# Down projections by seven products over 12 of 22 inner chunks, with squares at each eviction

## The chip, the cores and the metric

The kernel runs on one core of one Trainium2 chip. Its time is the device time of one execution in microseconds; less is better. The engines are TensorE (PE, with its weight loads as PEld), VectorE (DVE), ScalarE (ACT), GpSimd (POOL) and SyncE (SP), each of which takes its instructions in a fixed order from its own queue. DMAs are issued from the queues of SP and of POOL.

## The reference

A trunk of two layers over 512 tokens of width 1024, in float32:

```python
for i in range(DEPTH):                       # DEPTH = 2
    h = h + 0.5 * swiglu(rmsnorm(h, norm_ffn1[i]), ffn1_w_gate[i], ffn1_w_up[i], ffn1_w_down[i])
    hn = rmsnorm(h, norm_mix[i])
    h = h + (ab_mixer(hn, ...) if i % 2 == 0 else c_mixer(hn, ...))
    h = h + 0.5 * swiglu(rmsnorm(h, norm_ffn2[i]), ffn2_w_gate[i], ffn2_w_up[i], ffn2_w_down[i])
    gate = jax.nn.sigmoid(rmsnorm(h, norm_ple[i]) @ w_ple_gate[i])
    h = h + gate * (p[i] @ w_ple_proj[i])
return rmsnorm(h, norm_final)

def swiglu(x, w_gate, w_up, w_down):         # w_gate, w_up: 1024 x 2816, w_down: 2816 x 1024
    return (jax.nn.silu(x @ w_gate) * (x @ w_up)) @ w_down
```

The change is in the product with `w_down`, of which there are four (two in each layer), and in the RMS norm behind it.

## The kernel before

Activations lie transposed: a chunk is 128 features by 512 tokens, so `h` has 8 chunks (KC) and the inner activation of a feed-forward block 22 (NF). To keep float32 accuracy with the faster fp32r matmul, each operand is split into a high part (a copy rounded to fp32r, made by ACT) and a low part (the rest, made by DVE); `split` does this (L149, L150 for weights). A product is then three matmuls: high by high, high by low, low by high. Raw weights come by DMA into `wr` tiles; the split ones stand in the pools `whi` and `wlo`, of four buffers each, which set how far ahead weights can be prepared.

A feed-forward block computes its 22 inner chunks one after the other, with the gate and up products; the chunks' parts are kept in SBUF (the list `a`), and the raw chunks that the down projection needs again are written to DRAM (`raw`). Then `down` makes the 8 output chunks in four pairs m = 0, 2, 4, 6, every one over 22 inner chunks. The pair m = 0 is plain: 22 × 3 matmuls of 128x512 for each output chunk (L438 to L440). Beside it, `inner_sums` makes differences of inner chunks k and k + 4 for the later pairs (L515). The pairs 2, 4 and 6 treat the inner chunks 0 to 7 as 2 × 2 blocks (an output pair by two halves of 256 tokens) by a scheme of seven products in place of eight (Strassen's in Winograd's form). Its matmuls are 128x256 (L476 to L478); `inner_weights` makes the sums of weights on DVE (L529 to L533) and splits them. The products go to the banks p1, p2 (`mm`), y (`sc`) and z (`ob`); L490 to L494 combine y and z on DVE into two half results. The 14 other inner chunks are plain, behind the seven products, in each of these pairs.

At the end of an output chunk `evict` (L443) adds the PSUM bank to the residual on DVE and stores the new `h` to DRAM from POOL's queue (L444). For the next norm each chunk of `h` needs two things: its parts scaled by the gain (`norm_split`, L199 and L200), and its square (ACT, L207), which is added to the running sum `ssq` on POOL, or on DVE in the first norm and for the last chunk (L214). Chunks 3, 4 and 5 (LATER) were held back: SP fetches them again during the last pair, and both steps are done then.

At the very start `pair_front` does the first inner pairs of the first block, while the first norm is still being computed; PE sums `ssq` over partitions with one-column matmuls (L221), L223 and L224 make the inverse root of it, and L240 spreads it.

The order on each engine comes from a scheduler, which places the instructions by their dependences and its own estimates, in an order near that of the code; `issue_after` and `keep_in_program_order` tie single instructions.

Of the kernel before, what the change touches and what calls it, by code (L numbers as in the profile page):

```python
# [9 lines left out]
F32 = mybir.dt.float32  # L10
F32R = mybir.dt.float32r
# [4 lines left out]
P = 128  # L16
T = 512
# [19 lines left out]
SEVEN = 4  # L37
LATER = 3, 4, 5
UP_AT = 3
LEAD = 6  # L40
ACTS = 62
# [6 lines left out]
class Trunk:  # L48
# [155 lines left out]
    def norm_square(self, c):  # L204
# [5 lines left out]
        if c == 0:  # L210
            self.acc = sq
        else:
            eng = nc.vector if c == KC - 1 or self.k == 0 else nc.gpsimd
            eng.tensor_tensor(self.acc, self.acc, sq, op=ALU.add)  # L214
# [37 lines left out]
    def pair_front(self, w, m, first, ahead):  # L252
# [3 lines left out]
        for j in range(2):  # L256
            u = self.ahead.pop(0) if self.ahead else self.unit(w[:, (1 - j) * UNIT:(2 - j) * UNIT])
# [132 lines left out]
    def ffn(self, i, which, k_next):  # L390
# [8 lines left out]
        raw = self.dp.tile([2 * SEVEN, P, T], F32, name=self.nm("inner"))  # L399
        for m in range(NF):  # L400
# [6 lines left out]
            if m < 2 * SEVEN:  # L407
                nc.gpsimd.dma_start(raw[m], r)
# [9 lines left out]
    def down(self, w, a, raw, kept):  # L418

# [6 lines left out]
        later = []  # L426
# [6 lines left out]
        def plain(p, m, s, e, start):  # L433
            u = self.unit(w[m, :, s * P:e * P], (e - s) * P)
            for j, (xh, xl) in enumerate(a[s:e]):
# [4 lines left out]
                mm(p, u[1][:, c], xh, start=False, stop=s + j == NF - 1, skip_group_check=True)  # L440

        def evict(m, p, h):
# [10 lines left out]
        for s in range(0, NF, 8):  # L453
            for m in range(2):
                plain(ps[m], m, s, min(NF, s + 8), s == 0)
            if s == 0:
                sums = [self.inner_sums(k, a, raw) for k in range(SEVEN)]
# [3 lines left out]
        for m in range(2, KC, 2):  # L461
            hs = [fetched(m + j, kept) for j in range(2)]
            wa, wb, ws, wr = self.inner_weights(w[m, :, :UNIT], w[m + 1, :, :UNIT])
            M = UNIT // 2
            p1, p2, y, z = self.bank(), self.bank(), self.sbank(), self.obank()
            x11 = [(h[:, l], lo[:, l]) for h, lo in a[:SEVEN]]
            x21, x22 = [[(h[:, c], lo[:, c]) for h, lo in a[SEVEN:2 * SEVEN]] for c in (l, r)]
            t4 = [(h[:, r], lo[:, r]) for h, lo in a[:SEVEN]]
            t1, t2 = [[(h[:, c], lo[:, c]) for h, lo, _ in sums] for c in (l, r)]
            t3 = [(t[:, l], t[:, r]) for _, _, t in sums]  # L470

            def product(out, u, off, xs, start=False, stop=False):
                mm = nc.tensor.matmul
                for k, (xh, xl) in enumerate(xs):
                    c = slice(off + k * P, off + (k + 1) * P)
                    mm(out, u[0][:, c], xh, start=start and k == 0, stop=False, skip_group_check=True)  # L476
                    mm(out, u[0][:, c], xl, start=False, stop=False, skip_group_check=True)
                    mm(out, u[1][:, c], xh, start=False, stop=stop and k == SEVEN - 1, skip_group_check=True)  # L478

            e, f, u2 = self.tmp(), self.tmp(), self.tmp()  # L480
            product(y[:, l], wa, 0, x11, True)
            act(e[:, l], y[:, l], AF.Copy)
            product(p1[:, l], wa, M, x21, True)
            product(p2[:, l], wb, 0, t4, True)
            product(z[:, l], ws, M, t1, True, True)
            product(y[:, r], ws, 0, t3)
            product(p1[:, r], wr, M, x22)
            product(y[:, l], wr, 0, t2, False, True)
# [4 lines left out]
            for h, x in zip(hs, (e, f)):  # L493
                stt(h, x, 0.5, h, op0=ALU.mult, op1=ALU.add)  # L494
            if m == KC - 2:
                for c in later:
                    self.h[c] = fetched(c, self.kept)
                    self.norm_chunk(c)
            for j, p in enumerate((p1, p2)):
                for s in range(2 * SEVEN, NF, 8):  # L500
                    plain(p, m + j, s, min(NF, s + 8), False)
                evict(m + j, p, hs[j])

    def inner_sums(self, k, a, raw):
# [6 lines left out]
        nc.sync.dma_start(x2, raw[k + SEVEN])  # L511
# [9 lines left out]
    def inner_weights(self, w1, w2):  # L521

        nc, M = self.nc, UNIT // 2
        ra, rs = [self.wr.tile([P, UNIT], F32, tag="wr", name=self.nm("wr")) for _ in range(2)]
        nc.sync.dma_start(ra, w1)
        nc.sync.dma_start(rs, w2)
        tt = nc.vector.tensor_tensor
        wa, wb = self.parts(ra), self.parts(rs[:, M:])
        tt(rs[:, M:], rs[:, :M], rs[:, M:], op=ALU.add)  # L529
        tt(rs[:, :M], ra[:, :M], rs[:, :M], op=ALU.subtract)  # L530
        ws = self.parts(rs)
        tt(ra[:, :M], rs[:, M:], ra[:, :M], op=ALU.subtract)
        tt(ra[:, M:], ra[:, M:], ra[:, :M], op=ALU.subtract)  # L533
        return wa, wb, ws, self.parts(ra)

    def parts(self, raw):
        n = raw.shape[-1]
        hi = self.wh.tile([P, UNIT], F32R, tag="wh", name=self.nm("wh"))
        lo = self.wl.tile([P, UNIT], F32R, tag="wl", name=self.nm("wl"))
        self.split(raw, hi[:, :n], lo[:, :n])  # L540
        return hi, lo
# [883 lines left out]
```

## Time and profile before

| | us |
|---|---|
| median of 3 runs | 2041.67 |
| lowest and highest | 2040.91 and 2044.22 |
| the profiled execution | 2042.86 |
| its span | 2041.1 |

The profiled execution is 1.2 us over the median. Times in rows of the trace count from the start of its span. In a row of groups the last columns are the count, the busy time, the mean of one in ns, and the idle time ahead of them; in a row of waits, the total in us, how often, and the longest; in a row of the timeline, the start, the duration, what ran, and in brackets the idle time before it with what ended that.

The four down projections take about 117 us each: the first runs from 239.66 to 357.03.

### The profile page before, as it was taken

To read this page: it belongs to the slowest core of one execution; us is meant where nothing else is said; L and a number is where in the kernel's file an instruction comes from. 1 tells how busy PE (TensorE), PEld (TensorE's weight loads), DVE (VectorE), ACT (ScalarE), POOL (GpSimd) and SP (SyncE) were. 2 spreads that over 40 slices of the span, in tenths; PEclk is the share of its full clock that TensorE was granted. 3 is DMA by queue.
4 is the path that set the end of the run, shared out by engine and by line. 5 is a ranking of instruction groups with operands and counts; after the bars stand their busy time and mean duration, and the time that the engine had idled before them with its cause. 6 is when DMAs were issued, how large, how long until landed. Compare 5 with 4: busy or idle time off the path is not lost.

```text
span 2041.1 us, 33721 instructions
## 1 busy us (share of the span) xinstructions
PE 2019.5 (99%) x12862; PEld 1820.6 (89%) x12862; DVE 1520.3 (74%) x2575; ACT 1056.9 (52%) x1798; POOL 260.2 (13%) x294
## 2 busy tenths in 40 slices
PE   9999999999999999999999999999999999999997
PEld 6999988878888899988888999888888889998886
DVE  7888865598766988875668888756788688888554
ACT  6555533377644555552445555434666545555242
POOL 0100011342212110000211100002000111000021
PEclk9999999999999999999999999999999999999999
DMA  7777644553425576653545775645343447665451
GB/s 212 193 188 188 181 139 157 150 104 73 100 73 165 137 195 182 170 191 124 185 150 159 192 183 158 201 125 161 109 112 102 155 134 192 184 179 165 132 193 42
DMA packets 123123, 312.94 MB, mean 153 GB/s; under 512 B 23504, under 2 KB 31184, under 8 KB 122960
## 3 DMA queue, kind: packets, MB, share of 16 engines
q1 hardware_dynamic: 104064, 253.06, 38.3%
q0 software_dynamic: 18752, 57.69, 15.0%
q8 instruction: 101, 1.65, 0.3%
q14 instruction: 62, 0.51, 0.1%
q10 hardware_dynamic: 144, 0.04, 0.0%
HBM read 274.02 MB, written 25.66 MB: 147 GB/s over the span
## 4 chain that ended last, share of the span: by engine, by line
PE 90%; DVE 3%; DMA 2%; ACT 2%; issue 1%; POOL 1%; SPq 0%; DVEq 0%; POOLq 0%; ACTq 0%
PE mm L362 6%; PE mm L361 6%; PE mm L360 6%; PE mm L174 6%; PE mm L438 6%; PE mm L439 6%; PE mm L173 6%; PE mm L440 6%; PE mm L175 6%; PE sc L362 3%; PE sc L361 3%; PE sc L360 3%; PE sc L175 3%; PE sc L173 3%; PE sc L174 3%; PE ob L360 2%
## 5 line engine op out<-in xcount | busy, mean ns | idle before, releaser
L149 ACT ACTIVATE wh<-wr 128x1024 fp32r<-128x1024 f32 (+2 forms) x455 | 466.2, 1026 | 541.5 <-PE mm L439 170.7
L150 DVE TENSOR_TENSOR wl<-wr,wh 128x1024 fp32r<-128x1024 f32 (+2 forms) x455 | 542.8, 1196 | 203.6 <-ACT wh L149 198.1
L362 PE MATMUL mm<-act,wl 128*128 128x256 f32 x1088 | 307.9, 283 | 0.0
L361 PE MATMUL mm<-act,wh 128*128 128x256 f32 x1088 | 307.9, 283 | 0.0
L360 PE MATMUL mm<-act,wh 128*128 128x256 f32 x1088 | 307.9, 283 | 0.0
L173 PE MATMUL mm<-act,wh 128*128 128x512 f32 (+1 forms) x648 | 254.4, 393 | 0.9 <-ACT act L149 0.4
L174 PE MATMUL mm<-act,wh 128*128 128x512 f32 (+1 forms) x648 | 254.2, 392 | 0.7 <-DVE act L200 0.6
L175 PE MATMUL mm<-act,wl 128*128 128x512 f32 (+1 forms) x648 | 253.3, 391 | 0.0
L361 PEld LDWEIGHTS mm<-act,wh 128*128 128x128 f32 x1088 | 208.9, 192 | 0.4
L362 PEld LDWEIGHTS mm<-act,wl 128*128 128x128 f32 x1088 | 208.9, 192 | 0.2
L360 PEld LDWEIGHTS mm<-act,wh 128*128 128x128 f32 x1088 | 208.9, 192 | 0.2
L438 PE MATMUL mm<-act,wh 128*128 128x512 f32 x512 | 199.4, 389 | 0.0
L439 PE MATMUL mm<-act,wh 128*128 128x512 f32 x512 | 199.4, 389 | 0.0
L440 PE MATMUL mm<-act,wl 128*128 128x512 f32 x512 | 199.2, 389 | 0.0
L149 ACT ACTIVATE act<-tmp 128x512 fp32r<-128x512 f32 (+1 forms) x204 | 113.7, 590 | 83.0 <-DVE tmp L515 33.1
L360 PE MATMUL sc<-act,wh 128*128 128x256 f32 x544 | 154.0, 283 | 0.0
L361 PE MATMUL sc<-act,wh 128*128 128x256 f32 x544 | 154.0, 283 | 0.0
L362 PE MATMUL sc<-act,wl 128*128 128x256 f32 x544 | 154.0, 283 | 0.0
L174 PEld LDWEIGHTS mm<-act,wh 128*128 128x128 f32 x648 | 122.2, 189 | 24.5 <-DVE act L200 2.2
L173 PEld LDWEIGHTS mm<-act,wh 128*128 128x128 f32 x648 | 121.9, 188 | 23.9 <-ACT act L199 0.8
L175 PEld LDWEIGHTS mm<-act,wl 128*128 128x128 f32 x648 | 122.1, 188 | 22.1 <-DVE wl L150 0.2
L150 DVE TENSOR_TENSOR act<-tmp,act 128x512 fp32r<-128x512 f32 (+1 forms) x200 | 125.7, 643 | 9.7 <-ACT act L149 7.7
(224 smaller groups left out, 4430.0 us busy)
## 6 DMA issues: line engine op xcount, KB each, us to landing
wr<-in_gu_dram SPq DMA_DIRECT2D x176, 512.0 KB, 4.7
wr<-in_gu_dram POOLq DMA_DIRECT2D x68, 512.0 KB, 5.5
wr<-in_dn_dram SPq DMA_DIRECT2D x64, 512.0 KB, 3.9
rb<-in_gu_dram SPq DMA_DIRECT2D x68, 256.0 KB, 3.0
wr<-in_dn_dram SPq DMA_DIRECT2D x32, 384.0 KB, 3.2
wr<-in_qk_ab_dram SPq DMA_DIRECT2D x20, 512.0 KB, 3.3
tmp<-kept SPq DMA_DIRECT2D x36, 256.0 KB, 4.1
inner<-tmp POOLq DMA_DIRECT2D x32, 256.0 KB, 3.6
```

What stands on the lines that cost most here:

```text
L149: self.put(self.nc.scalar.activation(hi, src, AF.Copy))
L150: self.put((lo_eng or self.nc.vector).tensor_tensor(lo, src, hi.bitcast(F32), op=ALU.subtract))
L173: mm(out, stat[0], mov[0], start=start, stop=False)
L174: mm(out, stat[0], mov[1], start=False, stop=False)
L175: return mm(out, stat[1], mov[0], start=False, stop=stop)
L360: mm(out, w[0][:, c], xs[k][0][:, x], start=start and k == 0, stop=False, skip_group_check=True)
L361: mm(out, w[0][:, c], xs[k][1][:, x], start=False, stop=False, skip_group_check=True)
L362: mm(out, w[1][:, c], xs[k][0][:, x], start=False, stop=stop and k == half - 1, skip_group_check=True)
L438: mm(p, u[0][:, c], xh, start=start and j == 0, stop=False, skip_group_check=True)
L439: mm(p, u[0][:, c], xl, start=False, stop=False, skip_group_check=True)
L440: mm(p, u[1][:, c], xh, start=False, stop=s + j == NF - 1, skip_group_check=True)
```

## The change

The scheme of seven products now covers 12 inner chunks, paired as `TWO` says, and 10 stay plain. For each of the pairs m = 2, 4, 6 the matmuls of 128x256 go from 84 to 126, and those of 128x512 from 84 to 60. There are six sums in place of four, beside the pair m = 0, and 12 raw chunks are written to DRAM instead of 8. `inner_weights` loads a wide and a narrow part for each output chunk, the narrow one into tiles `rb`, and fills six split tiles where there were four. The pair m = 2 runs its plain chunks first and its seven products last; m = 4 and m = 6 run the seven first.

Chunks 1 to 5 are now held back, but only for their split; the square, and its addition to `ssq`, are made at every eviction. Before the seven products of m = 6 three of the held chunks are fetched from POOL's queue, the other two as they are needed.

In the first block the weights of the third inner pair are split behind the last addition of the first norm.

The diff, cut to its core:

```diff
+TWO = (0, 4), (1, 5), (2, 6), (3, 7), (8, 10), (9, 11)
-SEVEN = 4
-LATER = 3, 4, 5
+SEVEN = 12
+LATER = 1, 2, 3, 4, 5
+READY = 3
-ACTS = 62
+ACTS = 64
...
-    def unit(self, src, cols=UNIT, lo_eng=None):
+    def unit(self, src, cols=UNIT, lo_eng=None, behind=None):
...
-        self.split(raw[:, :cols], hi[:, :cols], lo[:, :cols], lo_eng)
+        with self.tc.issue_after(behind.ins) if behind else ExitStack():
+            self.split(raw[:, :cols], hi[:, :cols], lo[:, :cols], lo_eng)
...
-            eng.tensor_tensor(self.acc, self.acc, sq, op=ALU.add)
+            self.last_sum = eng.tensor_tensor(self.acc, self.acc, sq, op=ALU.add)
...
-            u = self.ahead.pop(0) if self.ahead else self.unit(w[:, (1 - j) * UNIT:(2 - j) * UNIT])
+            u = self.ahead.pop(0) if self.ahead else self.unit(
+                w[:, (1 - j) * UNIT:(2 - j) * UNIT], behind=self.last_sum if first and m == 2 else None)
...
-            if m < 2 * SEVEN:
+            if m < SEVEN:
                 nc.gpsimd.dma_start(raw[m], r)
...
+        def fetch_later(c):
+            self.h[c] = self.tmp()
+            nc.gpsimd.dma_start(self.h[c], self.kept[c])
+
         def evict(m, p, h):
             stt(h, p, 0.5, h, op0=ALU.mult, op1=ALU.add)
             nc.gpsimd.dma_start(self.kept[m], h)
             self.h[m] = h
-            if m in LATER:
-                later.append(m)
-            else:
-                self.norm_chunk(m)
+            if m not in LATER:
+                self.norm_split(m)
+            self.norm_square(m)
...
+        def seven(m, p1, p2, first, hs):
+            a11, a12, a22, s1, s2, s3, s4 = self.inner_weights(w[m], w[m + 1])
+            y, z = self.sbank(), self.obank()
+            product(y[:, l], a11, x11, True)
+            act(e[:, l], y[:, l], AF.Copy)
+            product(p1[:, l], a12, x21, first)
+            product(p2[:, l], a22, t4, first, not first)
+            product(z[:, l], s1, t1, True, True)
+            product(y[:, r], s3, t3)
+            product(p1[:, r], s4, x22, False, not first)
+            product(y[:, l], s2, t2, False, True)
...
+        for m in range(2, KC, 2):
+            hs = [fetched(m + j, kept) for j in range(2)]
+            ps = self.bank(), self.bank()
+            first = m > 2
+            if m == KC - 2:
+                for c in LATER[:READY]:
+                    fetch_later(c)
+            if first:
+                seven(m, *ps, True, hs)
+            if m == KC - 2:
+                for n, c in enumerate(LATER):
+                    if n >= READY:
+                        fetch_later(c)
+                    self.norm_split(c)
+            for j, p in enumerate(ps):
+                others(p, m + j, not first, first)
+                if first:
+                    evict(m + j, p, hs[j])
+            if not first:
+                seven(m, *ps, False, hs)
+                for j, p in enumerate(ps):
+                    evict(m + j, p, hs[j])
...
 def inner_weights(self, w1, w2):
+        for n, s in ((UNIT, 0), (M, UNIT)):
+            for x in (w1, w2):
+                raws.append(tile(self.wr, "wr", F32) if n == UNIT else
+                            self.tp.tile([P, T], F32, tag="rb", name=self.nm("rb"), bufs=2))
+                dma(raws[-1], x[:, s:s + n])
+        ra, rs, ra2, rs2 = raws
+        (ga,), (gb, b22) = parts(ra), parts(ra2, rs[:, M:])
...
+        (gs,) = parts(rs)
+        hi, lo = tile(self.wh, "wh", F32R), tile(self.wl, "wl", F32R)
+        self.split(rs2[:, G:], hi[:, :G], lo[:, :G])
+        tt(rs2[:, G:], rs2[:, :G], rs2[:, G:], op=ALU.add)
+        tt(rs2[:, :G], ra2[:, :G], rs2[:, :G], op=ALU.subtract)
+        self.split(rs2, hi[:, G:G + M], lo[:, G:G + M])
...
+        (gr,) = parts(ra)
...
+        (gr2,) = parts(ra2)
```

By the diff's insertions the lines move: the splits L149, L150 become L151, L152; the matmuls of the seven L476 to L478 become L481 to L483; L443 becomes L455, L214 L217, L221 L224.

Where the instructions stand after it, in three places of the first down projection and of the start. On DVE in the kernel before, between the sevens of m = 2 and m = 4, four low parts of plain weights (columns 1024 and 768) stood ahead of the work that ends the seven:

```order
L150 TENSOR_TENSOR wl_3392<-wr_3371,wh_3391 128x1024
L150 TENSOR_TENSOR wl_3495<-wr_3493,wh_3494 128x1024
L150 TENSOR_TENSOR wl_3525<-wr_3523,wh_3524 128x768
L150 TENSOR_TENSOR wl_3551<-wr_3549,wh_3550 128x1024
L150 TENSOR_TENSOR wl_3581<-wr_3579,wh_3580 128x768
L490 TENSOR_TENSOR tmp_3399<-ob_3398,tmp_3401 128x256
L491 TENSOR_TENSOR tmp_3400<-sc_3397,tmp_3401 128x256
```

On DVE now, the last of the rows between the seven of m = 2 and that of m = 4 (mm_3164 and mm_3165 are the banks of m = 2; wr_3448, rb_3452 and rb_3454 are raw weights of m = 4):

```order
L455 SCALAR_TENSOR_TENSOR tmp_3160<-mm_3164,tmp_3160 128x512
L503 SCALAR_TENSOR_TENSOR tmp_3162<-tmp_3297,tmp_3162 128x512
L152 TENSOR_TENSOR wl_3473<-rb_3454,wh_3472 128x256
L455 SCALAR_TENSOR_TENSOR tmp_3162<-mm_3165,tmp_3162 128x512
L576 TENSOR_TENSOR rb_3454<-rb_3454 128x256
L152 TENSOR_TENSOR wl_3483<-wr_3448,wh_3482 128x1024
L577 TENSOR_TENSOR rb_3454<-rb_3452,rb_3454 128x256
L583 TENSOR_TENSOR rb_3452<-rb_3454,rb_3452 128x256
L584 TENSOR_TENSOR rb_3452<-rb_3452 128x256
L152 TENSOR_TENSOR wl_3473<-rb_3454,wh_3472 128x512
```

The evictions of m = 2 now stand among the weights of m = 4, and no plain weights lie between the two sevens.

On POOL before, around the same place, the stores of chunks 2 to 5 and the addition of chunk 2's square:

```order
L444 DMA kept_2854<-tmp_3122 128x512
L214 TENSOR_TENSOR ssq_3111<-ssq_3111,tmp_3308 128x512
L444 DMA kept_2854<-tmp_3124 128x512
L444 DMA kept_2854<-tmp_3367 128x512
L444 DMA kept_2854<-tmp_3369 128x512
```

And now:

```order
L456 DMA kept_2858<-tmp_3160 128x512
L217 TENSOR_TENSOR ssq_3153<-ssq_3153,tmp_3434 128x512
L456 DMA kept_2858<-tmp_3162 128x512
L217 TENSOR_TENSOR ssq_3153<-ssq_3153,tmp_3439 128x512
L456 DMA kept_2858<-tmp_3442 128x512
```

Each store is now followed by the addition of its chunk's square.

On PE now, in the seven of m = 4, the place where the second pieces of wh_3472 and wl_3473 (512 columns, made from the sums in rb_3454) are first needed for z (`ob`) and for y's right half (`sc`); the first of these rows is the 72nd matmul of that seven:

```order
L483 MATMUL sc_3492<-act_2954,wl_3469 128x256
L481 MATMUL sc_3492<-act_2973,wh_3468 128x256
L482 MATMUL sc_3492<-act_2973,wh_3468 128x256
L481 MATMUL ob_3493<-act_3076,wh_3472 128x256
L482 MATMUL ob_3493<-act_3077,wh_3472 128x256
L483 MATMUL sc_3492<-act_2973,wl_3469 128x256
L481 MATMUL sc_3492<-act_2992,wh_3468 128x256
L482 MATMUL sc_3492<-act_2992,wh_3468 128x256
L483 MATMUL sc_3492<-act_2992,wl_3469 128x256
L481 MATMUL sc_3492<-act_3071,wh_3472 128x256
L483 MATMUL ob_3493<-act_3076,wl_3473 128x256
```

Matmuls of z and of y alternate there; the low part comes into use seven matmuls after the high part.

On DVE at the start before, around the last of the seven additions to `ssq` (wl_411 and wl_441 are low parts of the third inner pair):

```order
L214 TENSOR_TENSOR ssq_244<-ssq_244,tmp_261 128x512
L150 TENSOR_TENSOR wl_411<-wr_409,wh_410 128x1024
L214 TENSOR_TENSOR ssq_244<-ssq_244,tmp_264 128x512
L150 TENSOR_TENSOR wl_441<-wr_439,wh_440 128x1024
L223 TENSOR_SCALAR ms_273<-tr_268 128x4
```

And now:

```order
L217 TENSOR_TENSOR ssq_244<-ssq_244,tmp_264 128x512
L152 TENSOR_TENSOR wl_411<-wr_409,wh_410 128x1024
L226 TENSOR_SCALAR ms_273<-tr_268 128x4
L152 TENSOR_TENSOR wl_441<-wr_439,wh_440 128x1024
L807 TENSOR_SCALAR sink_4058<-sink_4058 128x12
```

The last addition now stands ahead of both low parts, and ms (the mean of squares) ahead of the second.

More of the change, by code (lines that the diff above doesn't have):

```diff
@@ L453, in down @@
         for s in range(0, NF, 8):
+            e = min(NF, s + 8)
             for m in range(2):
-                plain(ps[m], m, s, min(NF, s + 8), s == 0)
-            if s == 0:
-                sums = [self.inner_sums(k, a, raw) for k in range(SEVEN)]
+                plain(ps[m], m, s, e, s == 0, e == NF)
+            sums += [self.inner_sums(k, k2, a, raw) for k, k2 in TWO if s <= max(k, k2) < e]
         for m in range(2):
             evict(m, ps[m], hs[m])
[L461 to L478, printed above, removed]
@@ new lines, in down, with product @@
+        x11 = [tuple(x[:, l] for x in a[k]) for k, _ in TWO]
+        x21, x22 = [[tuple(x[:, c] for x in a[k]) for _, k in TWO] for c in (l, r)]
+        t4 = [tuple(x[:, r] for x in a[k]) for k, _ in TWO]
+        t1, t2 = [[(h[:, c], lo[:, c]) for h, lo, _ in sums] for c in (l, r)]
+        t3 = [(t[:, l], t[:, r]) for _, _, t in sums]
+        def product(out, us, xs, start=False, stop=False):
+            mm = nc.tensor.matmul
+            for k, (u, (xh, xl)) in enumerate(zip(us, xs)):
+                mm(out, u[0], xh, start=start and k == 0, stop=False, skip_group_check=True)
+                mm(out, u[0], xl, start=False, stop=False, skip_group_check=True)
+                mm(out, u[1], xh, start=False, stop=stop and k == len(xs) - 1, skip_group_check=True)
@@ L494, in down, with inner_sums @@
                 stt(h, x, 0.5, h, op0=ALU.mult, op1=ALU.add)
+        for m in range(2, KC, 2):
+            hs = [fetched(m + j, kept) for j in range(2)]
+            ps = self.bank(), self.bank()
+            first = m > 2
             if m == KC - 2:
[L496 to L504, printed above, removed]
+                for c in LATER[:READY]:
[15 more added lines that the diff above has]
+                    evict(m + j, p, hs[j])
+    def inner_sums(self, k, k2, a, raw):
         nc, H = self.nc, T // 2
@@ L521, in inner_weights @@
     def inner_weights(self, w1, w2):
[L523 to L528, printed above, removed]
+        nc, dma, tt = self.nc, self.nc.sync.dma_start, self.nc.vector.tensor_tensor
+        M, G = UNIT // 2, UNIT // 4
+        tile = lambda pool, tag, dt: pool.tile([P, UNIT], dt, tag=tag, name=self.nm(tag))
@@ new lines, in inner_weights, with parts @@
+        raws = []
+        for n, s in ((UNIT, 0), (M, UNIT)):
[4 more added lines that the diff above has]
+        ra, rs, ra2, rs2 = raws
+        def parts(*srcs):
+            hi, lo, out, n = tile(self.wh, "wh", F32R), tile(self.wl, "wl", F32R), [], 0
+            for x in srcs:
+                c = slice(n, n + x.shape[-1])
+                self.split(x, hi[:, c], lo[:, c])
+                out.append([(hi[:, i:i + P], lo[:, i:i + P]) for i in range(c.start, c.stop, P)])
+                n = c.stop
+            return out
@@ L532, in inner_weights @@
+        d22, d3, d1 = [[(hi[:, c + i:c + i + P], lo[:, c + i:c + i + P]) for i in range(0, G, P)] for c in (0, G, M)]
         tt(ra[:, :M], rs[:, M:], ra[:, :M], op=ALU.subtract)
         tt(ra[:, M:], ra[:, M:], ra[:, :M], op=ALU.subtract)
[L534 to L541, printed above, removed]
+        (gr,) = parts(ra)
```

26 lines of the change are left out of this document (13 added, 13 removed).

## The prediction

> **What bounds the kernel now.** I read the page first, then the list of what TensorE waits for, then a table of windows over the first down projection, one window for each output pair (m = 0, 2, 4, 6).
>
> ```profile
> span 2041.1 us, 33721 instructions
> PE 2019.5 (99%) x12862; PEld 1820.6 (89%) x12862; DVE 1520.3 (74%) x2575; ACT 1056.9 (52%) x1798; POOL 260.2 (13%) x294
> ...
> PE ob L664 <- ACT tmp L149: 1.7, 7, 0.3
> PE tr L1268 <- ACT tmp L1262: 1.7, 1, 1.7
> ...
> PE tr L221 <- DVE ssq L214: 1.0, 1, 1.0
> ```
>
> TensorE is busy 99% of the span, and the longest waits after its start add up to a few microseconds: none of these three rows is in a down projection. The windows (columns: sum and busy time of PE, weight loads, DVE, ACT, POOL, then the granted clock, the DMA share, GB/s) agree:
>
> ```profile
> 239.66:269.61 29.95, 29.95 (x134) 24.79 (x133) 24.39 (x45) 12.97 (x23) 0.58 (x1) 1.00 0.54 181
> 269.61:298.75 29.14, 29.14 (x169) 25.84 (x168) 17.54 (x21) 10.55 (x14) 4.68 (x4) 1.00 0.49 155
> 298.75:327.89 29.14, 29.14 (x169) 25.85 (x168) 15.09 (x19) 8.29 (x10) 1.10 (x2) 1.00 0.43 137
> 327.89:357.03 29.14, 29.14 (x169) 25.84 (x168) 18.61 (x19) 13.51 (x19) 7.43 (x6) 1.00 0.56 181
> ```
>
> PE fills every window, at full clock. So the time of a down projection is now its matmuls, and two things can change it: their number, and waits that do not exist yet. DVE is far from full as a mean (15 to 24 of 29 us), but a mean says nothing about one short stretch.
>
> **1. Fewer matmuls: −5.0 us.** In the rows of pair m = 2 the seven products run from 269.61 and the plain chunks from 279.68. Durations overlap, so I take start to start.
>
> ```profile
> 269.61 0.28 PE L476 MATMUL sc<-act,wh 128*128 128x256 f32 x1
> ...
> 279.56 0.28 PE L478 MATMUL sc<-act,wl 128*128 128x256 f32 x1
> 279.68 0.40 PE L438 MATMUL mm<-act,wh 128*128 128x512 f32 x1
> ...
> 298.52 0.39 PE L440 MATMUL mm<-act,wl 128*128 128x512 f32 x1
> 298.75 0.28 PE L476 MATMUL sc<-act,wh 128*128 128x256 f32 x1
> ```
>
> 84 half-width matmuls take 279.68 − 269.61 = 10.07 us, 0.120 each; 84 full ones 298.75 − 279.68 = 19.07, 0.227 each. With six pairs of chunks instead of four a seven has 7 × 6 × 3 = 126 half ones (+42), and 2 × 10 × 3 = 60 full ones remain (−24): +42 × 0.1199 − 24 × 0.2270 = −0.41 us for a pair; the three pairs of four down projections give 12 × −0.41 = **−5.0 us**. This is nearly certain, and it is all that the larger scheme can gain.
>
> **2. Two sevens back to back: a new wait, +8.8 us.** m = 2 now runs its plain chunks first and its seven last, m = 4 its seven first. Six split weight tiles serve a seven, and the pools whi and wlo have four buffers. So the first tile for m = 4 (wh_3456) waits until the seven of m = 2 has read the tile four before it, 42 matmuls or about 4.9 us before that seven ends. Call that end T0. ACT then splits (1.06), and DVE starts at about T0 − 3.7 and has no gap: 22 instructions up to the second piece of wl_3473, the low part that the seven of m = 4 needs. Start to start, by rows of the same kinds:
>
> ```profile
> 266.65 1.23 DVE L150 TENSOR_TENSOR wl<-wr,wh 128x1024 fp32r<-128x1024 f32 x1 [0.23 <-ACT wh L149]
> 267.79 0.75 DVE L200 SCALAR_TENSOR_TENSOR act<-tmp,gain,act 128x512 fp32r<-128x512 f32 x1
> ...
> 262.18 0.69 DVE L150 TENSOR_TENSOR wl<-wr,wh 128x512 fp32r<-128x512 f32 x1
> 262.90 0.69 DVE L529 TENSOR_TENSOR wr<-wr 128x512 f32<-128x512 f32 x1
> ...
> 281.52 0.42 DVE L490 TENSOR_TENSOR tmp<-ob,tmp 128x256 f32<-128x256 f32 x1
> 281.85 0.41 DVE L491 TENSOR_TENSOR tmp<-sc,tmp 128x256 f32<-128x256 f32 x1
> ...
> 265.55 1.06 ACT L149 ACTIVATE wh<-wr 128x1024 fp32r<-128x1024 f32 x1 [3.45 <-PE mm L439]
> ```
>
> Three 1024-wide low parts at 1.14 (3.4); seven 512-wide weight operations at 0.69 as a mean of dependent (0.72) and independent ones (4.9); the two L503 and two evictions at 0.61 (2.4); eight 256-wide ones at 0.33 to 0.42 (3.1). That is 13.8 us, so the low part is there at T0 + 10.1 and its high part, an ACT step earlier, at T0 + 9.2. PE, which begins m = 4 at T0, comes to its first high part after 74 half matmuls (8.9 us) and to its first low part after 81 (9.7). On its own this costs some **0.4 us** for each down projection; the eviction that must free p2's bank (0.2) lies inside it.
>
> But the squares are now made at each eviction, also for chunks 2 and 3, and their additions to ssq stand on POOL right beside this stretch. What an addition does to DVE is in three places:
>
> ```profile
> 291.37 0.75 DVE L200 SCALAR_TENSOR_TENSOR act<-tmp,gain,act 128x512 fp32r<-128x512 f32 x1
> 292.03 1.79 DVE L530 TENSOR_TENSOR wr<-wr,wr 128x512 f32<-128x512 f32 x1
> ...
> 291.56 1.71 POOL L214 TENSOR_TENSOR ssq<-ssq,tmp 128x512 f32<-128x512 f32 x1 [0.58 <-ACT tmp L207]
> ...
> L530 DVE TENSOR_TENSOR wr<-wr,wr 128x512 f32<-128x512 f32 x12 | 12.7, 1057 | 0.3
> ...
> L529 DVE TENSOR_TENSOR wr<-wr 128x512 f32<-128x512 f32 x12 | 8.3, 692 | 0.4
> ...
> 636.88 1.53 POOL L214 TENSOR_TENSOR ssq<-ssq,tmp 128x512 f32<-128x512 f32 x1 [3.71 <-ACT tmp L207]
> 637.17 0.68 DVE L697 TENSOR_TENSOR act<-mm,act 128x512 f32<-128x512 f32 x1
> ```
>
> An L530 that began during an addition took 1.79 us where L529 takes 0.69: 1.1 lost. An operation that reads PSUM (L697, from mm) beside one was not slowed. The addition for chunk 2 falls partly beside the eviction of chunk 3, which reads PSUM: I take 0.74, about two thirds. That for chunk 3 falls among low parts and rb operations: 1.1. So the weights come 1.8 us later, and PE waits 0.4 + 1.8 = 2.2 us; four times, **+8.8 us**. The bounds are 1.6 (both additions hidden) and about 4 × (0.4 + 2 × 1.71) = 15 (each stops DVE for its whole 1.71), which I do not take since the rows show 1.1.
>
> The Trainium skill (SBUF — State Buffer, "🔬 SBUF: two separate sides") calls the port pair that the two engines share an exclusive lock that whoever starts first holds for the whole instruction. By it the price would run from nothing, where DVE is first each time, to the whole addition; the 1.1 of 1.71 lies between.
>
> **3. Elsewhere in the down projections: nothing.** The other two transitions have the 60 full matmuls of plain chunks (13.6 us) between two sevens, which covers the same chain of 13.8 that starts 3.7 early; without that cover they would cost what part 2 costs. Two more sums in the m = 0 window are about 6 us of DVE (each four 256-wide differences and low parts of 1024 columns in all, some 3 us by the durations above) on 24.4 of 29.95: it just fits, and what spills falls into the plain chunks of m = 2. The store of four more raw chunks and the fetches ahead go through POOL's queue, busy 0.6 to 7.4 us of a window.
>
> **4. The start: −2.0 us.**
>
> ```profile
> 17.82 4.67 DVE L214 TENSOR_TENSOR ssq<-ssq,tmp 128x512 f32<-128x512 f32 x6
> 22.41 1.22 DVE L150 TENSOR_TENSOR wl<-wr,wh 128x1024 fp32r<-128x1024 f32 x1
> 23.54 0.68 DVE L214 TENSOR_TENSOR ssq<-ssq,tmp 128x512 f32<-128x512 f32 x1
> ...
> 24.28 1.05 PE L221 MATMUL tr<-ones,ssq 128*128 128x1 f32 x8 [1.00 <-DVE ssq L214]
> 25.20 0.48 PE L173 MATMUL mm<-act,wh 128*128 128x512 f32 x1
> ...
> 25.90:29.30 3.40, 3.40 (x12) 2.76 (x11) 0.31 (x1) 0.69 (x2) 0.73 (x1) 0.51 0.82 218
> ```
>
> The seventh addition stands behind a weight's low part of 1.1 us. With that behind it, it ends near 23.2 instead of 24.2. But PE now has L224 three matmuls (0.7 us) earlier, so it still waits 0.7 to 0.8: −0.3 us. After the old wait the clock was 0.51 for 3.4 us, which cost 3.4 × 0.49 = 1.7. A later stretch with 0.82 us of idle kept it:
>
> ```profile
> 1974.90:1978.30 3.40, 2.58 (x13) 1.55 (x12) 1.99 (x1) 1.38 (x2) 2.42 (x2) 1.00 1.02 324
> ```
>
> I take the shorter wait to keep it too: −0.3 − 1.7 = **−2.0**; the other end is −0.3.
>
> The Trainium skill (TensorE: Matmul & The Clock Gate, "🎯 Why this matters for your kernels") advises against idle gaps over about 3 us, an idle window being what halves the clock. By that rule the 1.0 us here should have cost no clock, and the waits of part 2 would cost none. The trace shows the opposite here, so the measurement decides.
>
> **5. The mixers and the last stage: 0 ± 2.** Order in part of the first mixer changes; its waits above are a microsecond or less each.
>
> **Sum.** −5.0 + 8.8 − 2.0 = +1.8 us, from a profiled run of 2042.86 (span 2041.1 and 1.8 around it) to 2044.7. The median of the runs is 2041.67, 1.2 below it, so the forecast is **2043.5**.
>
> **The rivals.**
> - *B, the additions stay clear of DVE.* They come a little earlier or later, or wait for DVE. Then part 2 is 1.6: −5.0 + 1.6 − 2.0 = −5.4, 2036.3. For it: the L697 row, and a slack in DVE of 10 us a window; against: DVE has no gap just there. Between it and mine, with one addition hidden, lies 2039.5 or so.
> - *C, the other side: the new waits halve the clock.* At the start a wait of 1.0 us and eight one-column matmuls were enough. The place is the middle of m = 4's seven; the price 1.7 each time; it decides once over half of the four trip, at some 2 us in one clock window. All four: +1.8 + 4 × 1.7 = +8.6, 2050.3. Against it: a wait may be cut in two by a matmul or two between high and low parts, or by a window's border.
> - *D, the start's clock drops as before:* +1.7, 2045.2.
>
> **How the numbers follow.** Mine, with D and one clock drop: 0.45 (2041 to 2047). B: 0.20; half of it: 0.15. C with two or more drops: 0.20. The range reaches from just below B, 2035, to C, 2050. A measurement of this kernel can tell about 0.2%, 4.1 us, from no change: faster (below 2037.6) takes B and some of the half, 0.25; slower (above 2045.8) takes C and the upper end of mine, 0.30; the same 0.45.
>
> **What would show it.** Part 1: 1512 half-width matmuls in the seven products, still 0.120 apart. Part 2: a row of PE's waits for DVE wl or ACT wh at L481 to L483, four times about 2 us, and rb operations of over 1 us beside POOL's L217. If these waits are below 0.5 us, B holds; if the windows after them show a clock near 0.5, C. Part 4: PE's wait at L224, and the clock from 25 to 29 us. I am wrong outright if waits show up at another transition, most likely after m = 0, or if the loads of weights come late.

## The result and the profile after

The changed kernel takes 2045.96 us (median of 22 runs, 2043.77 to 2049.31), against 2042.51 for the kernel before in runs beside it: a ratio of 1.0019, with a 95% interval of 1.0013 to 1.0024, so it is slower by some 3 to 5 us. One of the 22 runs of the kernel before was a slow one (2809.5 us), which the ratio leaves out. The forecast was 2043.5 in a range of 2035 to 2050, with a change too small to tell from none as the likeliest case (0.45).

The waits of TensorE in the changed kernel (line, what it waited for, total us, times, longest):

```profile
PE ob L481 <- ACT wh L151: 5.7, 4, 1.4
PE ob L710 <- ACT tmp L151: 1.9, 8, 0.3
PE tr L1314 <- ACT tmp L1308: 1.7, 1, 1.7
PE sc L177 <- POOL act L152: 1.6, 4, 0.8
PE tr L224 <- DVE ssq L217: 1.5, 1, 1.5
```

The first row is new: four waits of 1.4 us, one in each down projection, for the high part at the place that the prediction named. The first down projection as one window, from its first matmul to the first of the stage behind it, in the kernel before:

```profile
239.66:357.03 117.37, 117.37 (x638) 102.33 (x637) 75.62 (x104) 45.32 (x66) 13.78 (x13) 1.00 0.50 163
```

and in the changed kernel:

```profile
239.14:357.12 117.98, 116.56 (x692) 104.05 (x691) 87.69 (x141) 50.90 (x83) 15.97 (x18) 1.00 0.54 176
```

It became 0.6 us longer, with 1.4 us in which PE is idle. By the same windows over the whole program, the profiled span of 2044.3 us is 3.2 above that of before: the four down projections give 4 × 0.6 = +2.5; the start −0.5; the stage between the first and the second down projection +0.5; that behind the second +1.4; those behind the third and the fourth −0.1 and −0.5. Rows on DVE around the late high part, in the seven of m = 4 (start, us, what):

```profile
303.50 0.68 DVE L455 SCALAR_TENSOR_TENSOR tmp<-mm,tmp 128x512 f32<-128x512 f32 x1
304.10 1.02 DVE L576 TENSOR_TENSOR rb<-rb 128x256 f32<-128x256 f32 x1
305.04 1.21 DVE L152 TENSOR_TENSOR wl<-wr,wh 128x1024 fp32r<-128x1024 f32 x1
306.18 1.50 DVE L577 TENSOR_TENSOR rb<-rb,rb 128x256 f32<-128x256 f32 x1
307.71 0.43 DVE L583 TENSOR_TENSOR rb<-rb,rb 128x256 f32<-128x256 f32 x1
```

beside these rows on POOL:

```profile
303.52 1.31 POOL L217 TENSOR_TENSOR ssq<-ssq,tmp 128x512 f32<-128x512 f32 x1
304.76 0.56 POOL L456 DMA_DIRECT2D kept<-tmp  x1
305.33 2.06 POOL L217 TENSOR_TENSOR ssq<-ssq,tmp 128x512 f32<-128x512 f32 x1
```

The 256-wide operations L576, L577 and L583 do the same amount of work. L583, with nothing on POOL, takes 0.43 us; L576, which starts during the first addition, 1.02; L577, during the second, 1.50. That is 0.60 + 1.08 = 1.68 us. The eviction L455, which reads PSUM, and the 1024-wide low part, which had already begun when the second addition came, are not stretched. PE has its high part 1.4 us late:

```profile
306.70 0.28 PE L482 MATMUL sc<-act,wh 128*128 128x256 f32 x1
308.40 0.39 PE L481 MATMUL ob<-act,wh 128*128 128x256 f32 x1 [1.42 <-ACT wh L151]
```

### The profile page after: what moved, and what is told of

Read it like the earlier page. It is cut to its first block, busy times and chain, and to the rows that moved or that the text cites. A ratio compares the mean times of both kernels' runs of the same rounds, so it can differ in the third digit from the quotient of the medians.

```text
span 2044.3 us, 34597 instructions
## 1 busy us (share of the span) xinstructions
PE 2017.6 (99%) x13078; PEld 1828.8 (89%) x13078; DVE 1568.4 (77%) x2727; ACT 1079.2 (53%) x1870; POOL 278.8 (14%) x330
## 4 chain that ended last, share of the span: by engine, by line
PE 89%; DVE 4%; ACT 2%; DMA 2%; issue 2%; POOL 0%; SPq 0%; DVEq 0%; ACTq 0%; POOLq 0%
PE mm L366 6%; PE mm L365 6%; PE mm L364 6%; PE mm L177 6%; PE mm L176 6%; PE mm L178 6%; PE mm L441 4%; PE mm L442 4%; PE mm L443 4%; PE sc L366 3%; PE sc L365 3%; PE sc L364 3%; PE sc L176 3%; PE sc L178 3%; PE sc L177 3%
## 5 line engine op out<-in xcount | busy, mean ns | idle before, releaser
L151 ACT ACTIVATE wh<-wr 128x1024 fp32r<-128x1024 f32 (+3 forms) x455 | 454.7, 1002 | 443.3 <-DVE wr L354 81.4
L152 DVE TENSOR_TENSOR wl<-wr,wh 128x1024 fp32r<-128x1024 f32 (+3 forms) x455 | 527.9, 1164 | 161.1 <-ACT wh L151 153.6
L151 ACT ACTIVATE act<-tmp 128x512 fp32r<-128x512 f32 (+1 forms) x228 | 123.7, 578 | 111.0 <-DVE tmp L540 52.4
L441 PE MATMUL mm<-act,wh 128*128 128x512 f32 x416 | 162.0, 389 | 0.0
L442 PE MATMUL mm<-act,wh 128*128 128x512 f32 x416 | 162.0, 389 | 0.0
L443 PE MATMUL mm<-act,wl 128*128 128x512 f32 x416 | 161.8, 389 | 0.0
L152 DVE TENSOR_TENSOR act<-tmp,act 128x512 fp32r<-128x512 f32 (+1 forms) x224 | 136.8, 628 | 12.3 <-ACT act L151 9.0
```

Source lines behind the costliest of these rows:

```text
L151: self.put(self.nc.scalar.activation(hi, src, AF.Copy))
L152: self.put((lo_eng or self.nc.vector).tensor_tensor(lo, src, hi.bitcast(F32), op=ALU.subtract))
L441: mm(p, u[0][:, c], xh, start=start and j == 0, stop=False, skip_group_check=True)
L442: mm(p, u[0][:, c], xl, start=False, stop=False, skip_group_check=True)
L443: mm(p, u[1][:, c], xh, start=False, stop=stop and j == e - s - 1, skip_group_check=True)
```

## The experiments

Two theories stood against each other: that POOL's two additions stretch DVE's chain (theory 1), or that the chain behind four buffers is too long by itself (theory 2). Down projections below are the window of a whole one, as above, all four of a kernel within 0.03 us unless said otherwise. The last stage is what stands behind the second down projection of a layer: the gate, with the layer's extra input `p`. Ratios are to the kernel before, in runs beside each experiment.

**The squares of chunks 2 and 3 held back to m = 6.**

```diff
+HELD = 2, 3
...
-            self.norm_square(m)
+            if m not in HELD:
+                self.norm_square(m)
...
                     self.norm_split(c)
+                    if c in HELD:
+                        self.norm_square(c)
```

> The changed kernel, with the squares of chunks 2 and 3 (and their additions to ssq on POOL) held back to the seven products of m = 6; all else as changed. Theory 1 (the two additions slow DVE's rb operations through the two engines' shared access to SBUF, by 0.6 and 1.1 us, and that is the wait): TensorE's wait at L481 falls from 4 x 1.4 us to under 0.3 each, L576 and L577 take about 0.42 us, the 252 matmuls of the sevens of m = 2 and m = 4 run in 30.3 us instead of 32.0, the down projection takes 116.3 us instead of 118.0, and the time is 5 to 7 us below the changed kernel's, about 2 us below the kernel before. Theory 2 (the chain behind four buffers is too long by itself): the wait stays above 1 us each and the time changes by less than 2 us. If the four moved additions disturb m = 6, a new wait there shows it.

The waits at L481 are gone, and the down projections take 116.3 us: theory 1 as expected, theory 2 not. But the time is 2046.79 us, 1.0017 of the kernel before (1.0008 to 1.0026), no better than the changed kernel. No wait showed in m = 6; the loss came behind it. The stages behind the first three down projections take 0.7, 1.3 and 0.9 us more than in the changed kernel, and the last stage of the second layer takes 75.6 us instead of 70.8. The first waits of PE there are:

```profile
1975.69 0.49 PE L177 MATMUL sc<-act,wh 128*128 128x512 f32 x1 [0.71 <-ACT act L152]
...
1977.05 0.50 PE L178 MATMUL sc<-act,wh 128*128 128x512 f32 x1 [0.86 <-POOL act L153]
...
1978.93 0.61 PE L178 MATMUL sc<-act,wh 128*128 128x512 f32 x1 [0.86 <-POOL act L153]
```

PE waits there for the two parts of an extra input, and from 1978.93 to 1985.7 matmuls of 512 columns take 0.61 to 0.63 us instead of 0.39 to 0.50, which is the halved clock; by an estimate from its 6.8 us in the trace it cost up to 3.4 us. ACT's splits of this input in turn waited for its transfer:

```profile
1975.01 0.63 ACT L152 ACTIVATE act<-tmp 128x512 fp32r<-128x512 f32 x1 [3.33 <-DMA tmp<-in_pT_dram]
1976.89 0.63 ACT L152 ACTIVATE act<-tmp 128x512 fp32r<-128x512 f32 x1 [1.25 <-DMA tmp<-in_pT_dram]
```

The transfer was issued 0.8 us after the end of the down projection, where it had been 0.5 us ahead of it in the kernel before. Its buffers come from the same eight `tmp` tiles as the squares; that these were what it waited for was not tried by itself.

**The seven products of m = 2 ahead of its plain chunks.**

```diff
-            first = m > 2
+            first = True
```

> The changed kernel with the seven products of m = 2 ahead of its plain chunks, as m = 4 and m = 6 have them, so that plain chunks lie between any two sevens. Both theories of the wait expect the wait at m = 4 to go, 1.7 us for each down projection. The rival is that it only moves: the seven of m = 2 then follows m = 0 directly, and DVE must make six sums and the weights of m = 2 in 30 us, where it had 24.4 us of work before and gets about 6 more, so a wait of 0 to 3 us for wl or for the sums may stand ahead of m = 2. Without it the time is about 6 to 7 us below the changed kernel's; with 2 us there, as the changed kernel.

The rival held. There is no wait at m = 4 any more, but one or two at m = 2; the four down projections take 119.3, 117.4, 118.1 and 117.3 us, and the time is 2045.30 us, 1.0017 (1.0008 to 1.0026).

```profile
276.89 0.39 PE L483 MATMUL mm<-act,wl 128*128 128x256 f32 x1 [1.01 <-DVE wl L152]
...
280.94 0.39 PE L483 MATMUL ob<-act,wl 128*128 128x256 f32 x1 [1.27 <-DVE wl L152]
```

The time of the plain chunks ahead of m = 2 is thus what its preparation needs.

**One of six weight tiles in buffers of its own.**

```diff
-        (gr2,) = parts(ra2)
+        nh, nl = [p.tile([P, M], F32R, tag=t, name=self.nm(t), bufs=1) for p, t in ((self.wh, "wh2"), (self.wl, "wl2"))]
+        self.split(ra2, nh, nl)
+        gr2 = [(nh[:, i:i + P], nl[:, i:i + P]) for i in range(0, M, P)]
-ACTS = 64
+ACTS = 62
```

> The changed kernel with the last, half-wide tile of split weights of a seven in buffers of its own (one high, one low, 512 columns), so that five tiles instead of six go through the four buffers of whi and wlo; the room comes from two act tiles fewer (62). The first weights of m = 4 can then be split some 1 us and more earlier, while the additions stay where they are. If buffers and additions together make the wait (theory 1 with the chain of the prediction), the wait at L481 falls from 1.4 us to 0 to 0.5 each and the time by 4 to 6 us. If the additions alone decide, whatever the start of the chain, it stays near 1.4. If 62 act tiles are too few, new waits show elsewhere.

The wait stayed (5.4 us in all), and a second one joined it; 2050.09 us, 1.0038 (1.0025 to 1.0051). This run doesn't separate the theories as it was meant to. Measured against the start of m = 4, the chain did begin 1.6 us earlier, but two things ate it. The scheduler, which orders by its own estimates, now put the first use of that high part behind 66 matmuls instead of 74 (1.0 us earlier), and the second addition fell on a larger operation:

```profile
301.50 1.04 DVE L576 TENSOR_TENSOR rb<-rb 128x256 f32<-128x256 f32 x1
302.46 2.68 DVE L152 TENSOR_TENSOR wl<-wr,wh 128x1024 fp32r<-128x1024 f32 x1
```

The low part took 2.68 instead of 1.22 us, so the stretch is 2.1 us here. 1.0 + 0.4 against 1.6 leaves the wait nearly as it was. A shorter chain is no help as long as the order spends it.

The second wait is 0.3 to 0.4 us long and comes five matmuls behind the first. The first and the third down projection take 118.3 us, but the second and the fourth 119.9 and 119.8, because there the clock is halved for 3.41 us behind the two waits. The windows ahead of that and with it:

```profile
944.83:948.24 3.41, 1.75 (x13) 1.35 (x11) 3.32 (x6) 0.63 (x1) 0.11 (x1) 1.00 0.33 64
948.24:951.65 3.41, 3.29 (x15) 3.29 (x16) 1.10 (x3) 0.90 (x2) 0.00 (x0) 0.50 0.88 287
1924.46:1927.87 3.41, 1.78 (x13) 1.43 (x12) 2.88 (x6) 1.09 (x2) 0.00 (x0) 1.00 0.51 151
1927.87:1931.28 3.41, 3.41 (x18) 3.41 (x17) 1.52 (x2) 1.40 (x3) 0.00 (x0) 0.50 0.86 252
```

This is rival C of the prediction, in two of four down projections of this run, at 1.6 and 1.5 us each. Why not in the other two is told in the last section. The 1.6 us more in the stage behind the first down projection were not traced.

**Without the tie at the start.**

```diff
-                w[:, (1 - j) * UNIT:(2 - j) * UNIT], behind=self.last_sum if first and m == 2 else None)
+                w[:, (1 - j) * UNIT:(2 - j) * UNIT], behind=None)
```

> The changed kernel without the tie of the third inner pair's splits to the last square's addition. If that edit is worth what the two traces show at the start (the inner products end 0.5 us earlier with it), the time rises by 0 to 1 us, the wait at L224 falls from 1.5 to 1.0 us, and the clock is near 0.5 from 26 to 29 us. If the edit lengthens the start (its wait is longer), the time falls by about 0.5. The rival of the prediction, that the shorter wait would have kept the clock, is already against the trace.

2045.22 us, 1.0018 (1.0009 to 1.0027): like the changed kernel within the interval. The down projections are unchanged (118.0); the start is 0.6 us shorter, not longer, with full clock and a wait of 0.7 us at L224. The start is looked at once more below.

**The squares of chunks 2 and 3 behind the seven of m = 4.** As the first experiment, but placed there:

```diff
                 seven(m, *ps, True, hs)
+            if m == 4:
+                for c in HELD:
+                    self.norm_square(c)
```

> The changed kernel with the squares of chunks 2 and 3 made behind the seven products of m = 4 instead of at their eviction, so that their two additions run beside the plain chunks of m = 4, where DVE has idle time, and not beside the seven of m = 6 as with the first experiment. Theory 1 (contention of these two additions with DVE makes the wait): the wait at L481 goes, each down projection takes 116.3 us, and, since nothing is moved towards the next stage, the stages behind take what they take in the changed kernel: a span 6.7 us below the changed kernel's, about 2037.6. Rival (what is saved in the down projection is lost again in the stage behind it, because that stage waits for transfers of its own): the down projections take 116.3 us, but the stages behind grow as they did in the first experiment and the time stays within 2 us of the changed kernel's.

2039.42 us, 0.9987 (0.9979 to 0.9996). The span is 2037.7 where 2037.6 was expected; that it agrees to 0.1 us is in part luck, since the stage behind the second down projection took 287.0 us instead of 285.7 (the clock is at half from 1001.99 for 3.41 us), and the start and the last stage gave 1.2 us back. The stretch over both sevens, in the profile of this run:

```profile
281.90:312.15 30.25, 30.25 (x252) 30.15 (x251) 20.66 (x34) 11.35 (x18) 1.10 (x2) 1.00 0.46 137
```

252 matmuls in 30.25 us without an idle moment, as against 32.06 in the changed kernel; the down projections take 116.3. So the position of two squares and their additions, with the same work in all and PE's order up to the high part unchanged (it stands behind 74 matmuls here too), decides between 1.0019 and 0.9987.

**Every addition to ssq on DVE.**

```diff
-            eng = nc.vector if c == KC - 1 or self.k == 0 else nc.gpsimd
+            eng = nc.vector
```

> The changed kernel with every addition to ssq on DVE instead of POOL. In the order on DVE the two additions then stand inside the chain ahead of the high part that TensorE waits for: two times about 0.61 us of work of its own, instead of 1.68 us of stretching. Theory 1: L576 and L577 take 0.42 us, the wait at L481 falls by about 0.4 us to some 1.0, the down projection takes 117.5 us; with that the additions are shown to cost DVE less when DVE makes them itself. If the wait stays at 1.4 us or grows, the stretching was not from POOL.

2039.50 us, 0.9985 (0.9977 to 0.9994), with no wait at L481: better than expected. The groups of L576 and L577 over the whole changed kernel:

```profile
L577 DVE TENSOR_TENSOR rb<-rb,rb 128x256 f32<-128x256 f32 x12 | 9.4, 784 | 0.3
...
L576 DVE TENSOR_TENSOR rb<-rb 128x256 f32<-128x256 f32 x12 | 7.5, 624 | 0.3
```

and with the additions on DVE:

```profile
L576 DVE TENSOR_TENSOR rb<-rb 128x256 f32<-128x256 f32 x12 | 5.1, 422 | 0.3
L577 DVE TENSOR_TENSOR rb<-rb,rb 128x256 f32<-128x256 f32 x12 | 5.0, 420 | 0.1
```

The stretching was from POOL: here the squares and the evictions stand in the program where the changed kernel has them, and only the engine of the additions differs. What was missed: the additions as DVE's own work (0.60 us each, start to start) stand in the chain too, but the order now has ten more matmuls of other products ahead of the high part's first use, which comes after 84 instead of 74. That is 1.2 us, the time of the two additions. It looks as if the scheduler covers the work that it counts, while the stretching, which it does not seem to count, became a wait in full; its estimates themselves are not known, so this stays an inference.

**Candidates for a faster kernel.** The placement behind m = 4's seven, without the tie, and with the low parts of the last stage's extra input on DVE:

```diff
-            p.append(self.split_chunk(raw))
+            p.append(self.split_chunk(raw, nc.vector))
```

> A candidate for a faster kernel: the changed kernel with the squares of chunks 2 and 3 behind the seven of m = 4, without the tie of the third pair's splits, and with the low parts of the last stage's extra input made on DVE instead of POOL (0.69 instead of 1.28 us, in a place where TensorE waits for them). By theory 1 the down projections give 4 x -1.1 us against the kernel before; the last edit takes some 0.5 us off each of the waits at the beginning of the two last stages. Together 5 to 7 us below the kernel before. By the rival, which expects the stages behind to give it back, within 2 us of it.

2037.88 us, 0.9982 (0.9973 to 0.9990): 3.9 us below the kernel before, less than the 5 to 7 expected. Then with the additions on DVE as well:

> The same candidate with all additions to ssq on DVE too. DVE is free beside the plain chunks of m = 4, so there the additions cost nothing; theory 1 expects the same 116.3 us for a down projection and no stretched operations of DVE anywhere in it, and a time like that of the candidate before, within 2 us. Where the additions on DVE stand ahead of weights that TensorE waits for, new waits of about 0.6 us each would show.

2036.88 us, 0.9978 (0.9969 to 0.9987): the fastest by its median, 4.9 us under the kernel before and about 9 under the changed one, though its interval overlaps that of the candidate before. The stage behind the second down projection takes 284.4 us in both, as in the kernel before (284.3), and not 285.7 as in the changed kernel.

**The last four runs.** The changed kernel once more:

> The changed kernel itself once more, for a second profile of it beside the other runs of this group. All theories expect the four waits at L481 (1.4 us each) and down projections of 118.0 us again. What stays open is the start: if the clock there depends on where TensorE's wait falls against a period of its own, the clock from 22 to 29 us may this time be full, with the start shorter by 1 to 1.5 us; if it depends on the program, it is near 0.7 again.

2046.03 us; four waits of 1.4 us and down projections of 118.0 again. The clock at its start was 0.51 (below), and the start is not shorter than in the kernel before: 239.7.

The kernel before with the tie alone (the diff of `unit`, `norm_square` and `pair_front` from the change):

> The kernel before with one part of the change alone: the third inner pair's splits behind the last square's addition. The prediction held that to be worth 2.0 us by a clock that stays full; the runs so far show the start at 238.1 to 239.1 us with the tie and 238.4 to 239.7 without, and a clock that drops or not in either. By this the time is that of the kernel before, within 1 us; by the prediction, 2 us less.

2042.55 us, 1.0004 (0.9995 to 1.0012): nothing that can be told from no change, and not the prediction's −2 us.

The kernel before with the additions, and the low parts of the extra input, on DVE:

> The kernel before with two edits of the best candidate, without the larger scheme: all additions to ssq on DVE, and the low parts of the last stage's extra input on DVE. Here the down projections have no wait that the additions could cause, so they stay at 117.4 us; the last stages lose 0.5 us of a wait each. 0 to 1.5 us below the kernel before. The difference to the candidates is then what the larger scheme brings without its wait: 4 x 1.08 us by the windows.

2039.79 us, 0.9990 (0.9981 to 0.9999), a little more than expected; the down projections stay at 117.4. The last stages of the two layers are 0.5 and 1.5 us shorter.

The changed kernel with both of these edits and without the tie, no square held back:

> The changed kernel with all additions to ssq on DVE at each eviction (none held back), without the tie at the start, and with the low parts of the last stage's extra input on DVE. The additions then stand in the chain of m = 4, but as DVE's own work that the order allows for: as in the run with the additions alone, no wait at L481, 116.3 us for a down projection, and a time 4 to 6 us below the kernel before, like the best candidate so far. If it is slower than that by more than a microsecond, holding the two squares back is worth something of its own.

2038.59 us, 0.9982 (0.9973 to 0.9992), with 116.3 for a down projection: 3.4 us below the kernel before where 4 to 6 were expected. Its interval overlaps that of the fastest candidate, so what holding two squares back adds, once no addition is on POOL, is not settled.

Nor is it settled what the larger scheme itself is worth. The kernel before, with the two edits on DVE and without the scheme, takes 2039.79 us. The two candidates that have both edits and the scheme are 1.2 and 2.9 us below that by their medians, with overlapping intervals, and not the 4 × 1.08 = 4.3 us that the windows of the down projections give.

## Why the prediction came out as it did

The forecast of +1.8 us had the sign, and what came lay inside its range; the measured +3.5 to +4 is its double. By its parts:

1. **Fewer matmuls, −5.0 us.** Right but for 0.7: without the wait a down projection takes 116.3 instead of 117.4, which is 4 × −1.08 = −4.3. The half-width matmuls are the 378 in each that were expected, still 0.120 us apart. The remainder of 0.16 us in each lies in the pair m = 4 (28.89 us without the wait, against 28.71 and 28.74 for m = 2 and m = 6); its cause was not traced.
2. **The new wait, +8.8 us.** Mechanism and place were right, with its size too large: 118.0 − 116.3 = 1.7 us for each, +6.8. Two terms were off. The stretch of 1.84 us was 0.60 + 1.08 = 1.68. And the 0.4 us of the chain without additions was nothing: in the run with the additions behind the seven of m = 4, the high part is done 8.9 us after that seven begins, not 9.2, which is just when PE comes to it, after 74 matmuls. So there was no wait, and no slack either, and the whole stretch became loss. Rival B, additions that stay clear of DVE, was wrong for this kernel, but is what two of the experiments made of it: its 2036.3 came as 2039.4 and 2039.5.
3. **Elsewhere in the down projections nothing.** Right: no other wait there. The start of m = 2 is near its limit, as the second experiment showed.
4. **The start, −2.0 us.** This step failed. The wait at L224 was 1.5 us, not 0.7 to 0.8, since the additions began 0.3 us later than before and end at 23.6 instead of 23.2, and PE comes to L224 at 22.2, 1.1 us earlier than before where the prediction had 0.7 (the order has it four matmuls earlier, not three); and the clock dropped nevertheless. In 14 profiles the first down projection begins at 238.8 us on average with the tie (8 profiles) and 239.1 without (6), each group ranging over 1.7 to 2.0 us; the clock drops in 3 of 8 and in 3 of 6. The tie alone measured 1.0004. So this term was about −0.5 in the first profile, +0.04 in the second of the same kernel, and nothing that can be told as a mean. Sorted by the clock instead, the same 14 profiles begin the first down projection at 238.4 us on average without a drop (8) and at 239.7 with one (6); without a drop it is 238.4 with the tie and without it. The 1.3 us between the two include that the waits with a drop are longer, so the drop itself costs less than the 1.7 assumed, and the tie is worth as good as nothing. That −2.0 came from reading one profile's clock as the program's property.
5. **Mixers and the last stages, 0 ± 2.** The sum held (+1.3), but it hid +1.4 us in the last stage of the first layer, behind the second down projection (+0.8 in the second profile). PE waits there for parts of the extra input that POOL makes (L152, 0.85 us once); the rest was not traced. With these parts on DVE that wait is gone in all three candidates. In two of them the stage is as short as in the kernel before; in the third it takes 285.2 us, with a new wait of 0.6 us for ACT.

The rest follows: −4.3 + 6.8 − 0.5 + 1.3 is, but for rounding, the +3.2 of the profile. That the forecast came within 3 us is in part luck: the wait was put 2.0 us too high and the start 1.5 too low, and the two misses nearly cancel. Rival D, the start's clock dropping as before, is what the first two profiles of the changed kernel show, and its 2045.2 is the number nearest to the result. Rival C, the new waits halving the clock, did not happen in the changed kernel: the clock stays at 1.00 through its down projections. It did in two of the four with the separate buffers.

The Trainium skill (SBUF — State Buffer, "🔬 SBUF: two separate sides") says that a DVE operation with two SBUF inputs and a GpSimd operation that reads SBUF exclude each other, and that the one which began first keeps the ports. The exclusion agrees with the rows: L577 began 0.85 us into the second addition and was done at 307.68, 0.29 us after the addition's end at 307.39, and L576 was done at 305.12, 0.29 us after the first addition's end at 304.83. Who is first shows less well, and the profile's spans on POOL are rough. In the changed kernel the low part that began at 305.04, 0.29 us ahead of the second addition, was not touched, and the addition took 2.06 us instead of 1.31. But in the run with the separate buffers the low part that began at 302.46 was stretched by 1.46 us, though the second addition there began at 302.74, 0.28 us behind it by the records, and took 1.31.

## What to carry to other kernels

When TensorE is full, price a change by the one chain that ends last at each new place, and look at what runs beside that chain on other engines: two operations of 1.3 us on an idle engine cost 1.7 us in each down projection here, and moving them to the right place, or making them on the busy engine itself, was worth 6.5 us. Here the order covered the work that stood in it, but not the contention, which turned into a wait in full, and a chain that began earlier was spent by the next order. A loss that vanishes from one stage has to be looked for in the next: the first experiment removed the whole wait and gained nothing. And before a clock seen in one profile is priced as the program's, it has to be seen in several.

## What was not expected of the hardware

The clock at the start is not decided by the length of PE's wait alone. The windows before and behind that wait, in the run with the squares held back to m = 6 (wait 1.6 us), then in the second run of the changed kernel (1.5 us), then in the first candidate (1.1 us); the clock is the third number from the end:

```profile
22.40:25.80 3.40, 1.86 (x12) 1.73 (x13) 3.29 (x5) 0.91 (x1) 0.52 (x1) 1.00 0.29 60
25.80:29.20 3.40, 2.63 (x14) 1.89 (x14) 1.24 (x4) 0.60 (x1) 1.41 (x1) 1.00 0.88 275
```

```profile
22.40:25.80 3.40, 1.96 (x13) 1.76 (x14) 3.29 (x5) 0.81 (x1) 0.63 (x1) 0.99 0.27 48
25.80:29.20 3.40, 3.09 (x10) 2.17 (x9) 0.78 (x3) 0.60 (x1) 1.31 (x1) 0.51 0.90 277
```

```profile
22.40:25.80 3.40, 2.29 (x14) 1.75 (x13) 3.29 (x6) 0.39 (x1) 0.10 (x1) 1.00 0.45 123
25.80:29.20 3.40, 3.40 (x13) 2.71 (x12) 0.65 (x2) 1.02 (x2) 0.91 (x1) 0.62 0.82 232
```

The longest wait of the three kept the full clock, and the shortest lost it. The traces show where the difference lies. Leaving out the first and the last 10 us of the program, a stretch at half clock is 3.41 us long in every profile that has one (in one place two follow each other), and two in the same profile begin a whole multiple of 3.413 us apart: 948.24 and 1927.87 in the run with the separate buffers, 287 of them. So in each profile the clock changes on a grid of its own, which can be counted back to the start. In all six profiles with a drop there, the whole wait, of 1.0 to 2.1 us, lies between two borders of the grid, and the half clock begins at the second. In the run with the squares held back to m = 6 a border at 23.34 cuts the wait (22.36 to 23.94) into 1.0 and 0.6 us:

```profile
19.93:23.34 3.41, 2.43 (x11) 1.69 (x9) 2.91 (x5) 3.38 (x5) 0.00 (x0) 1.00 0.88 297
23.34:26.75 3.41, 2.55 (x14) 1.94 (x14) 3.07 (x5) 0.00 (x0) 1.47 (x1) 1.00 0.27 63
```

In the other seven profiles the wait is 0.7 to 0.9 us. The same shows in the run with the separate buffers: where the first wait and at least 0.28 us of the second lie between the same two borders, the clock drops; in the first down projection a border falls between the two, in the third it cuts the first, and the clock stays. A wait of 1.4 us by itself, whole between two borders, kept the clock in the third down projection of the changed kernel:

```profile
1348.78:1352.19 3.41, 1.99 (x17) 1.79 (x16) 3.16 (x6) 1.44 (x3) 1.28 (x1) 1.00 0.71 207
```

At the start less was enough, but there eight one-column matmuls follow the wait (0.9 us), which the busy time of PE counts. Where exactly the limit lies was not measured.

The Trainium skill (TensorE: Matmul & The Clock Gate, "🔬 Part 1: The HAM clock gate (the "warmup" mystery)") describes a window of 3413 ns that runs freely; the grid of 3.413 us agrees with it. That a whole idle window is needed for a drop, as the Trainium skill has it on the same page in "🎯 Why this matters for your kernels", does not fit: a wait of 1.0 us was enough in the kernel before.
